# Cached attention: four sequences in one score tile, one score bank for the prompt's heads, a smaller descriptor ring

## The chip, the cores and the metric

The kernel runs on one core of a Trainium2 chip. The time is device microseconds (us) of one execution; the kernel is run several times and the median counts. One further execution was recorded by the hardware profiler; all rows below come from it.

The core's engines are named as in the profile: PE (TensorE's matrix products) and PEld (its weight loads), DVE (VectorE), ACT (ScalarE), POOL (GpSimd) and SP (SyncE, which here only starts transfers). Each runs its own list of instructions in the order in which the program wrote it, and they wait for each other by semaphores.

## The reference, cut to what matters

One step of a decoder layer for 512 prompt positions and for 8 sequences of 8 new positions each, 576 rows in all. A combined projection makes queries, keys, values, forget gates and the inputs of a convolution; attention with a bias from the forget gates and the convolution follow, then an output projection, an MLP and a gated embedding. The change touches the attention of the eight sequences, which reads 2048 cached positions each, through a table of pages of 128 positions:

```python
D_MODEL, SEQ, DEC_BATCH, DEC_SEQ, PAST_LEN, PAGE_SIZE = 2048, 512, 8, 8, 2048, 128
N_HEADS, HEAD_DIM = 8, 128
...
def fox_attention_sample(q, k_new, v_new, logf_new, k_past, v_past, logf_past):
    lp = logf_past.astype(jnp.float32)
    r_past = (lax.cumsum(lp, axis=1, reverse=True) - lp).transpose(0, 2, 1)
    cn = jnp.cumsum(logf_new, axis=1).transpose(0, 2, 1)
    s_past = jnp.einsum('bqhd,bkhd->bhqk', q, k_past).astype(jnp.float32) * scale
    s_past = s_past + cn[..., :, None] + r_past[..., None, :]
    s_new = jnp.einsum('bqhd,bkhd->bhqk', q, k_new).astype(jnp.float32) * scale
    s_new = s_new + cn[..., :, None] - cn[..., None, :]
    causal = jnp.arange(T)[None, :] <= jnp.arange(T)[:, None]
    s_new = jnp.where(causal, s_new, -jnp.inf)
    p = jax.nn.softmax(jnp.concatenate([s_past, s_new], axis=-1), axis=-1).astype(v_new.dtype)
    return (jnp.einsum('bhqk,bkhd->bqhd', p[..., :P], v_past)
            + jnp.einsum('bhqk,bkhd->bqhd', p[..., P:], v_new))
...
    k_past = cache_k[l][page_table].reshape(dec_b, past, N_HEADS, HEAD_DIM)
    v_past = cache_v[l][page_table].reshape(dec_b, past, N_HEADS, HEAD_DIM)
    lf_past = cache_logf[l][page_table].reshape(dec_b, past, N_HEADS)
    attn = fox_attention_sample(q, k, v, logf, k_past, v_past, lf_past)
```

The prompt's own attention is causal over its 512 positions with the same kind of bias; each head's result is normalised over its 128 channels before the output projection. All inputs are 32-bit floats.

## The kernel before

The program has two phases. Phase 2 (MLP, gate and final norm) is not touched; it and the output projection ahead of it begin at about 853 us. Phase 1 makes the combined projection and does everything else in its gaps.

**The projection.** `gemm_tile` makes one tile of 128 output channels for 576 rows: its weights come as four blocks of 128x512 (256 KB, tile `wraw`), are split into a high and a low part (`whi`, `wlo`) and go through 96 matrix products of 128x288 into a double bank `U` (`mm6`, L495). It pauses eight times; a stretch between two pauses, 12 products, is called a half here. At every pause `half()` (L367) is called. It first runs `flush_later()` (instructions held back on purpose, mainly exponentials on ACT), then lets the side work go one step: the queue `side` (convolution, `conv_norm`, the first `finish`) at every half, `att` (the prompt's heads, one after the other) at odd halves, and at even halves a credit grows by `DEC_RATE`; whenever it passes 1, the cached attention goes one step. So about every fourth half has a cache step. When the tiles are through, a drain loop alternates what is left with the projection of the embedding (`ple`, L1126).

**The cached attention** (`decode`, L795) has 16 units: two groups g of four heads, times eight sequences b. A unit has four steps, one for a chunk c of 512 positions (four pages). Rows of a score tile are 32 per head, of which eight (the sequence's queries) are meant; the other 24 hold queries of neighbours and are not used. A step issues, in this order:

- four transposes of the previous step's probabilities `dp` into bank `T` (L825), which ACT copies, eight columns of 32 only, to a 128x128 tile `PTs` (L826);
- a product of a selector `selU` with the table `R` (L838), which writes the bias of the 512 positions into bank `S`; the selector of the next unit is made by ACT at every fourth step (`unit_selector`, L871);
- 16 products of the queries `q_s` (as 32-column weights) with the cached keys `k`, added into `S` (L842);
- DVE's read of `S`, which adds the query's own bias, writes `dp` and gives the row maximum (L846), and its negation (L848); the exponential on ACT is put on `later` (L850);
- transfers on the SP queue for steps ahead (`load`, L802): two key tiles and two value tiles of 512 KB, each as two transfers of 256 KB with the page number read from the table. Five key tiles and four value tiles can be held;
- 16 products (32 records in the profile) of `PTs` with the cached values `v` of the step before the previous one, into a quarter of bank `O` (L863).

At a unit's last step `unit_end` (L877) merges the four chunks by their maxima, a 128x128 sum `uoc`, and POOL writes it to memory (`oc`, L892). The generator takes 66 steps.

**`finish(g)`** (L894) adds the eight new positions for a group of four heads: scores in bank `S` or `O`, their softmax, one transpose, products with the new values `v_s` for each sequence by itself (32 per round of four, L964), the merge with `oc` read back from memory, the norm, transposes of each sequence's 128x128 result (L984), and ACT's eight-column copies to `att_s` (L986). For g = 0 this goes in two rounds of four sequences beside the projection, for g = 1 in one round of eight in the drain.

**The prompt's heads** (`prompt_head`, L714): for each of four query blocks, `scores` (three products into `S`, DVE's read, a late exponential), `turned` (transposes to `T`, ACT's copy `pT`) and `values` (products into `S`, read twice by ACT, L752 and L753). It pauses nine times, once per odd half.

PSUM, the matrix products' memory, has eight banks of 128x512: two for `S`, one for `T`, one for `O`, two pairs for `U`.

Of the kernel before, what the change touches and what calls it, by code (L numbers as in the profile page):

```python
# [28 lines left out]
DEC_RATE = 0.485  # L29
# [6 lines left out]
C_ID, C_SELH, C_UM, C_CM, C_BM = 0, 128, 256, 272, 280  # L36
C_KEEP = 288
C_TRIU, C_SLOW, C_MASK = 288, 416, 544
C_SELG = 672
C_SEL16 = C_SELG + 256  # L40
# [3 lines left out]
C_T2 = C_TRIS + 32  # L44
C_END = C_T2 + 64


def const_pack():
# [8 lines left out]
    for r in range(128):  # L57
        h4 = r % 4
        c[r, C_SELH + h4 * 32:C_SELH + h4 * 32 + 32] = 1.0
        c[r, C_UM + r // 8] = 1.0  # L60
        g = C_SELG + r // 64 * 128 + h4 * 32
        c[r, g:g + 32] = 1.0
# [5 lines left out]
    q = p % 32  # L68
    for k in range(8):
        c[:, C_CM + k] = np.where((q < 8) & (k <= q), 0.0, NEG)  # L70
    for r in range(64):
        for qq in range(8):
            c[r, C_TRIS + qq] = (r % 8) <= qq
        c[r, C_BM + r // 8] = 1.0
        for k in range(64):
            c[r, C_T2 + k] = (r % 8) <= (k % 8)
# [66 lines left out]
class Kern:  # L143
# [28 lines left out]
    def row_rsqrt(self, ps, pool, dg, acc, out, n):  # L172
# [13 lines left out]
        for o, m in ((0, 512), (512, 64)):  # L186
            yield
            nc.tensor.matmul(pt[:, :m], self.ones, dg[:, o:o + m], start=True, stop=True)
            nc.scalar.activation(out[:, o:o + m], pt[:, :m], AF.Copy)
# [19 lines left out]
    heads = keys = 0  # L209
# [4 lines left out]
    def build(self):  # L214
        tc, nc, a = self.tc, self.nc, self.a
        with ExitStack() as top:
# [8 lines left out]
            self.oc = [dram.tile([128, 8, 128], F32, name=f"oc{j}") for j in range(2)]  # L225
# [17 lines left out]
    def phase1(self):  # L243
# [10 lines left out]
        ps_, pt_, po_, pu = Q("ps", 2), Q("pt", 1), Q("po", 1), Q("pu", 2)  # L254
# [3 lines left out]
        O_ = lambda: po_.tile([128, 512], F32, name="O", tag="O")  # L258
        U_ = lambda: pu.tile([128, 2, 512], F32, name="U", tag="U")
        self.S_, self.T_, self.O_, self.U_ = S_, T_, O_, U_  # L260

# [38 lines left out]
        self.selH, self.um, self.cm, self.bm = kc(C_SELH, 128), kc(C_UM, 16), kc(C_CM, 8), kc(C_BM, 8)  # L300
# [40 lines left out]
        self.att_s = c1.tile([128, 8, 64], F32, name="att_s")  # L341
        self.ysum = c1.tile([128, NR], F32, name="ysum")
        self.mlu = c1.tile([128, 2, 16], F32, name="mlu")
        self.PTs = []
        for i in range(2):
            t = c1.tile([128, 152], F32, name=f"PTs{i}")
            nc.gpsimd.memset(t[:, 128:], 0.0)
            self.PTs.append(t)
        self.PTm = c1.tile([64, 4, 56], F32, name="PTm")
        nc.gpsimd.memset(self.PTm, 0.0)  # L350
# [16 lines left out]
        def half():  # L367
# [8 lines left out]
            step(side)  # L376
            if odd:
                step(att)
                return
            D["credit"] += DEC_RATE  # L380
            if D["credit"] >= 1.0:
                D["credit"] -= 1.0
                if next(D["dec"], self) is self and D["mid"] is None:
# [3 lines left out]
                    side.append(self.finish(1, O_, O_, D["mid"]))  # L387
# [74 lines left out]
        while att or fq:  # L462
# [3 lines left out]
            step(att)  # L466
            next(ple, None)
            if n != 4:
                step(fq)
# [57 lines left out]
    def f_proj(self, wf, bfb):  # L527
# [57 lines left out]
        LBv = LB.rearrange("p (g h) b -> p g h b", g=2)  # L585
        LD = sm.tile([64, 2, 8, 2, 4], F32, name="LD")
# [24 lines left out]
        for h in range(4):  # L611
            nc.tensor.matmul(t[32 * h:32 * h + 32, :16].rearrange("p (g b) -> p g b", g=2), cp[:64, C_TRIS:C_TRIS + 32],
                             LBv[:, :, h, :], start=True, stop=True)
        self.cns = c1.tile([128, 16], F32, name="cns")
        nc.vector.tensor_copy(self.cns, t[:, :16])
        t = self.S_()
        nc.tensor.matmul(t[:, :64], LD.rearrange("p g b i h -> p (g b i h)"), cp[:64, C_T2:C_T2 + 64], start=True, stop=True)
        self.Rn = c1.tile([128, 64], F32R, name="Rn")
# [1272 lines left out]
```

## Time and profile before

| what | us |
| --- | --- |
| median of three runs | 2761.66 (2754.88 to 2769.64) |
| span of the profiled execution | 2757.2 |
| start, first projection tiles, biases: 0 to 119 | 119.0 |
| projection with cached attention and heads: 119 to 745 | 626.0 |
| last tiles, first `finish`, last cache steps: 745 to 812 | 67.0 |
| drain with the last `finish`: 812 to 853.2 | 41.2 |
| output projection and phase 2: 853.2 to the end | 1904.0 |

The span is the profiled execution's own time; it lies 4.5 us below the median of the runs. The mean clock granted to TensorE is 0.99 of full speed in the last stage and 1.00 in the others. In that last stage the DMA engines moved 167 GB/s and were busy for 0.54 of the time; in the stage from 119 to 745 us it was 291 GB/s and 0.87.

A row of a group names line, engine, operation, output and inputs, shape and count, then busy time in us and the mean of one in ns, then the engine's idle time just before these instructions and what ended most of it. In a timeline row the first number is the start and the second the duration. A matrix product's duration holds the latency of the pipeline, so that two neighbours overlap in the list; the distance of their starts is what the first one costs.

### The profile page before, as it was taken

To read this page: it belongs to the slowest core of one execution; us is meant where nothing else is said; L and a number is where in the kernel's file an instruction comes from. 1 tells how busy PE (TensorE), PEld (TensorE's weight loads), DVE (VectorE), ACT (ScalarE), POOL (GpSimd) and SP (SyncE) were. 2 spreads that over 40 slices of the span, in tenths; PEclk is the share of its full clock that TensorE was granted. 3 is DMA by queue.
4 is the path that set the end of the run, shared out by engine and by line. 5 is a ranking of instruction groups with operands and counts; after the bars stand their busy time and mean duration, and the time that the engine had idled before them with its cause. 6 is when DMAs were issued, how large, how long until landed. Compare 5 with 4: busy or idle time off the path is not lost.

```text
span 2757.2 us, 57342 instructions
## 1 busy us (share of the span) xinstructions
PE 2692.2 (98%) x22217; PEld 2599.2 (94%) x22217; DVE 2094.4 (76%) x3718; ACT 1211.7 (44%) x1841; POOL 524.1 (19%) x927
## 2 busy tenths in 40 slices
PE   8999999999999999999999999989999999998997
PEld 8988889998888999999999999989999999998997
DVE  5677777766555447888888888889888888887676
ACT  4233334345644324444444444545444444444554
POOL 1177776731100000000000000100000000000110
PEclk9999999999999999999999999999999999999999
DMA  4688888988736455444444444665565665655675
GB/s 153 211 285 293 279 291 289 296 296 303 267 130 202 141 201 178 141 140 142 143 143 142 140 137 142 213 173 169 163 191 156 175 175 166 184 171 180 198 243 172
DMA packets 239332, 538.44 MB, mean 195 GB/s; under 512 B 25842, under 2 KB 26739, under 8 KB 239059
## 3 DMA queue, kind: packets, MB, share of 16 engines
q1 hardware_dynamic: 171410, 329.06, 37.0%
q0 software_dynamic: 34112, 144.75, 16.7%
q10 hardware_dynamic: 33536, 60.96, 6.9%
q8 instruction: 174, 2.85, 0.4%
q14 instruction: 100, 0.81, 0.1%
HBM read 442.67 MB, written 92.01 MB: 194 GB/s over the span
## 4 chain that ended last, share of the span: by engine, by line
PE 51%; issue 4%; DVE 2%; DMA 1%; ACT 0%; POOL 0%; DVEq 0%; ACTq 0%; POOLq 0%
PE P L1539 15%; PE P L1540 15%; PE P L1541 15%; PE P L1607 2%; PE P L1609 2%; PE P L1608 2%; DVE w2l L152 1%; DMA xs<-x 1%; DMA x<-c 0%; ACT w2h L149 0%; DVE xs L1478 0%; DVE w2r L1763 0%; DVE x L1595 0%; DVE w2r L1764 0%; DVE w2r L1762 0%
## 5 line engine op out<-in xcount | busy, mean ns | idle before, releaser
L1539 PE MATMUL P<-xs,w2h 128*128 128x288 f32 x3584 | 1065.3, 297 | 15.2 <-DVE c L1656 6.8
L1540 PE MATMUL P<-xs,w2h 128*128 128x288 f32 x3584 | 1062.8, 297 | 4.2 <-DVE xs L152 4.2
L1541 PE MATMUL P<-xs,w2l 128*128 128x288 f32 x3584 | 1058.7, 295 | 2.5 <-DVE w2l L152 2.5
L149 ACT ACTIVATE w2h<-w2r 128x896 fp32r<-128x896 f32 (+1 forms) x632 | 556.1, 889 | 718.8 <-PE P L1540 416.8
L152 DVE TENSOR_TENSOR w2l<-w2r,w2h 128x896 fp32r<-128x896 f32 (+1 forms) x632 | 637.4, 1011 | 215.1 <-ACT w2h L149 213.5
L1539 PEld LDWEIGHTS P<-xs,w2h 128*128 128x128 f32 x3584 | 677.0, 189 | 20.7 <-DVE c L1656 9.4
L1540 PEld LDWEIGHTS P<-xs,w2h 128*128 128x128 f32 x3584 | 678.4, 189 | 6.6 <-DVE xs L152 6.3
L1541 PEld LDWEIGHTS P<-xs,w2l 128*128 128x128 f32 x3584 | 677.6, 189 | 4.3 <-DVE w2l L152 4.0
L495 PE MATMUL U<-xh,whi 128*128 128x288 f32 x1792 | 400.8, 305 | 2.6 <-ACT whi L123 1.3
L495 PE MATMUL U<-xh,wlo 128*128 128x288 f32 x1792 | 384.0, 296 | 1.7 <-DVE wlo L129 1.7
L495 PE MATMUL U<-xl,whi 128*128 128x288 f32 x1792 | 383.4, 295 | 1.8 <-DVE xl L328 1.7
L495 PEld LDWEIGHTS U<-xh,whi 128*128 128x128 f32 x1792 | 287.6, 189 | 23.4 <-issue 16.9
L495 PEld LDWEIGHTS U<-xl,whi 128*128 128x128 f32 x1792 | 287.9, 188 | 2.8 <-DVE xl L328 2.8
L495 PEld LDWEIGHTS U<-xh,wlo 128*128 128x128 f32 x1792 | 288.1, 188 | 2.4 <-DVE wlo L129 2.4
L123 ACT ACTIVATE whi<-wraw 128x512 fp32r<-128x512 f32 x224 | 141.2, 630 | 279.4 <-PE U L495 146.3
L129 DVE TENSOR_TENSOR wlo<-wraw,whi 128x512 fp32r<-128x512 f32 x224 | 160.3, 716 | 94.7 <-ACT whi L123 93.4
L1036 DVE SCALAR_TENSOR_TENSOR y<-ue,cv,y 128x512 f32<-128x512 f32 x240 | 183.4, 764 | 4.2
L1762 DVE TENSOR_TENSOR w2r<-w2r 128x512 f32<-128x512 f32 (+1 forms) x273 | 177.5, 650 | 4.9 <-DMA w2r<-in_w_down 4.9
L1037 POOL TENSOR_SCALAR cvt<-us,cv 128x64 f32<-128x64 f32 x240 | 168.5, 702 | 21.8
L1607 PE MATMUL P<-xs,w2h 128*128 128x288 f32 x512 | 151.8, 297 | 1.1 <-ACT c L1655 1.1
L1609 PE MATMUL P<-xs,w2l 128*128 128x288 f32 x512 | 151.0, 295 | 1.1 <-DVE w2l L152 1.0
L1608 PE MATMUL P<-xs,w2h 128*128 128x288 f32 x512 | 150.8, 295 | 0.0
(378 smaller groups left out, 2978.6 us busy)
## 6 DMA issues: line engine op xcount, KB each, us to landing
k<-in_cache_kv SPq DMA_DIRECT2D x256, 256.0 KB, 4.9
v<-in_cache_kv SPq DMA_DIRECT2D x256, 256.0 KB, 4.6
w2r<-in_w_up SPq DMA_DIRECT2D x127, 512.0 KB, 4.0
w2r<-in_w_down SPq DMA_DIRECT2D x112, 512.0 KB, 4.0
wraw<-in_w_main ACTq DMA_DIRECT2D x156, 256.0 KB, 5.0
xs<-di POOLq DMA_DIRECT2D x32, 1008.0 KB, 6.1
w2r<-in_w_gate SPq DMA_DIRECT2D x60, 512.0 KB, 4.4
x<-c POOLq DMA_DIRECT2D x48, 576.0 KB, 7.2
```

The lines of the kernel that those rows point to most:

```text
L149: self.nc.scalar.activation(out, in_, AF.Copy, **kw)
L152: self.nc.vector.tensor_tensor(out, in_, f(hi), ALU.subtract)
L495: self.nc.tensor.matmul(u[:, r, :HR], w, x[:, r * HR:(r + 1) * HR], start=first and n == 0, stop=last and n == 2)
L1036: nc.vector.scalar_tensor_tensor(y, ue[:, j:j + NPR], w, y, ALU.mult, ALU.add)
L1037: nc.gpsimd.tensor_scalar(t, us[:, :, j:j + 8], w, None, ALU.mult)
L1539: nc.tensor.matmul(o, hi[:, ia, :], s.hi[:, ib, :], start=(i == 0), stop=False)
L1540: nc.tensor.matmul(o, hi[:, ia, :], s.lo[:, ib, :], start=False, stop=False)
L1541: nc.tensor.matmul(o, lo[:, ia, :], s.hi[:, ib, :], start=False, stop=(i == n - 1))
L1607: nc.tensor.matmul(o, hi[:, ia, :], s.hi[:, kh, rows], start=first and kh == 0, stop=False)
L1608: nc.tensor.matmul(o, hi[:, ia, :], s.lo[:, kh, rows], start=False, stop=False)
L1609: nc.tensor.matmul(o, lo[:, ia, :], s.hi[:, kh, rows], start=False, stop=last and kh == 1)
L1762: lambda: V(w[:, :, 4:6, :], w[:, :, 0:1, :].broadcast_to([128, m, 2, 128]), w[:, :, 1:3, :], ALU.add),
```

## The change

**Four sequences share a score tile.** A step still has the keys of 512 positions and one group of four heads, but they are one page each of four sequences (key tiles) and four pages of the running group's sequences (value tiles). Four steps fill one tile of a bank `D` of their own: `q_s` is laid out with zeros between the sequences (160 columns for four of them), so that 32 columns of weights place one sequence's eight queries in its eight rows of a head's 32 and add nothing to the other rows. Selector, DVE's read, exponential, transposes and ACT's copies (now all 512 columns, `PT`) stand only in every fourth step; keys and values are multiplied in every step as before. There are four groups of (four heads, four sequences) with four chunks each; the generator takes 68 steps. The value products add four steps' worth into the four quarters of `O`; `merge` then takes from each quarter the rows of one sequence (a mask `rm`) into an accumulator in SBUF, `oacc`, scaled by a running maximum and sum `mlu`. There are no spills to memory.

**`finish`** works on 2 x 256 columns for both groups of sequences at once: scores in 16 columns, two transposes before the values, 16 records of products with `v_s`, two transposes after it. Both calls have the same form; g = 1 uses the banks `D` and `O`. `PTs`, `PTm`, `selG`, `unit_selector` and `unit_end` are gone; the four selectors `selU` are made once in `small_operands`.

**The prompt's heads** have one bank `S` instead of two (the other is `D`). They are advanced at every half instead of every odd one; most pauses are doubled, and `values` comes one pause later than `turned` and `scores` of its round. The transpose of `v_s` goes to `T`, and `pT` has two buffers. The drain loop advances them twice per pass.

**The rest.** `DEC_RATE` goes from 0.485 to 0.495. The program's scratch for the descriptors of the transfers that POOL starts is set to 8192 bytes; before, the default stood. The past bias uses `D` and `O` in turn, and `row_rsqrt` takes a new bank for each of its two products.

```diff
-DEC_RATE = 0.485
+DEC_RATE = 0.495
...
-        ps_, pt_, po_, pu = Q("ps", 2), Q("pt", 1), Q("po", 1), Q("pu", 2)
+        ps_, pt_, po_, pd_, pu = Q("ps", 1), Q("pt", 1), Q("po", 1), Q("pd", 1), Q("pu", 2)
...
-        self.q_s = c1.tile([128, 8, 88], F32, name="q_s")
-        nc.gpsimd.memset(self.q_s[:, :, 64:], 0.0)
+        self.q_s = c1.tile([128, 8, 2, 160], F32, name="q_s")
+        nc.gpsimd.memset(self.q_s, 0.0)
...
             step(side)
+            step(att)
             if odd:
-                step(att)
                 return
             D["credit"] += DEC_RATE
...
-                    side.append(self.finish(1, O_, O_, D["mid"]))
+                    side.append(self.finish(1, D_, O_))
...
             step(att)
+            self.flush_later()
             next(ple, None)
+            step(att)
             if n != 4:
...
+        self.selU = c1.tile([128, 4, 128], F32R, name="selU")
+        for i in range(4):
+            nc.scalar.activation(self.selU[:, i, :], self.selH, AF.Copy, scale=self.um[:, i:i + 1])
...
+    def q_of(self, h, b):
+        o = b % 4 * 32
+        return self.q_s[:, h, b // 4, o:o + 32]
...
         scores(0)
-        yield
+        for _ in range(2):
+            yield
         turned(0)
         scores(1)
-        yield
+        for _ in range(2):
+            yield
...
-        t = self.S_()
+        t = self.T_()
         nc.tensor.transpose(t[:64, :128], v[:, NPR:], self.ident)
         nc.scalar.activation(self.v_s[:, h, :], t[:64, :128], AF.Copy)
         self.heads += 1
-        yield
+        for _ in range(2):
+            yield
         for qt in range(4):
-            values(qt, vn)
             if qt < 3:
                 turned(qt + 1)
             if qt < 2:
                 scores(qt + 2)
+            yield
+            values(qt, vn)
             if qt == 3:
...
-                g, b = n // 64, n // 8 % 8
+                G, c, w, j = n // 32, n // 8 % 4, n // 2 % 4, n % 2
                 t = dec.tile([128, 2, 4, 128], F32, name="kv"[i], tag="kv"[i] * 2, bufs=(5, 4)[i])
-                for j in range(2):
-                    e = b * NPG + n % 8 * 2 + j
+                for x in range(2):
+                    b, pg = (w, 2 * j + x) if i == 0 else (2 * j + x, w)
+                    e = (G % 2 * 4 + b) * NPG + c * 4 + pg
                     r = nc.sync.value_load(self.pti[0:1, e:e + 1])
-                    nc.sync.dma_start(t[:, j].rearrange("p h c -> p (h c)"),
-                                      a["cache_kv"][bass.ds(r, 1), g, :, 512 * i:512 * i + 512].rearrange("o p c -> p (o c)"))
+                    nc.sync.dma_start(t[:, x].rearrange("p h c -> p (h c)"),
+                                      a["cache_kv"][bass.ds(r, 1), G // 2, :, 512 * i:512 * i + 512].rearrange("o p c -> p (o c)"))
...
-        for n in range(66):
+        s = o = mu = p = None
+        al, ls = {}, {}
+        one = lambda name: sm.tile([128, 1], F32, name=name, tag=name)
+        for n in range(68):
             if n == 0:
                 load(0, 5)
-                selU = {0: self.unit_selector(0)}
                 yield
-            if 1 <= n < 65:
-                m = n - 1
+            sc, w = n // 4, n % 4
+            G, c = sc // 4, sc % 4
+            if n >= 4 and w == 0:
                 t = self.T_()
                 for i in range(4):
-                    nc.tensor.transpose(t[:, i * 128:i * 128 + 128], ps[m][:, i * 128:i * 128 + 128], self.ident)
-                nc.scalar.activation(self.PTs[m % 2][:, :128].rearrange("p (a q) -> p a q", q=8),
-                                     t.rearrange("p (a q) -> p a q", q=32)[:, :, :8], AF.Copy)
-                del ps[m]
+                    nc.tensor.transpose(t[:, i * 128:i * 128 + 128], p[:, i * 128:i * 128 + 128], self.ident)
+                for i, m in ((0, 128), (128, 512)):
+                    nc.scalar.activation(self.PT[:, i:m], t[:, i:m], AF.Copy)
             if n < 64:
-                u, c = n // 4, n % 4
-                g, b = u // 8, u % 8
-                if c == 0:
-                    mx = sm.tile([128, 4], F32, name="dmx", tag="dmx")
-                    l4 = sm.tile([128, 4], F32, name="dl4", tag="dl4")
-                    units[u] = [mx, l4, None]
-                mx, l4, _ = units[u]
-                s = self.S_()
-                nc.tensor.matmul(s, selU[u], self.R[:, c * 512:c * 512 + 512], start=True, stop=False)
+                if w == 0:
+                    s = self.D_()
+                    nc.tensor.matmul(s, self.selU[:, G, :], self.R[:, c * 512:c * 512 + 512], start=True, stop=False)
                 for i in range(2):
                     kt = tiles[0][2 * n + i]
                     for h in range(4):
                         nc.tensor.matmul(s[32 * h:32 * h + 32, i * 256:i * 256 + 256].rearrange("p (a b) -> p a b", a=2),
-                                         self.q_s[:, 4 * g + h, b * 8:b * 8 + 32], kt[:, :, h, :],
-                                         start=False, stop=(i == 1))
-                p = ps[n] = dec.tile([128, 512], F32, name="dp", tag="dp", bufs=2)
-                nc.vector.tensor_scalar(p, s, self.cns[:, u:u + 1], None, ALU.add, ALU.max, accum_out=mx[:, c:c + 1])
-                nm = sm.tile([128, 1], F32, name="dnm", tag="dnm")
-                nc.vector.tensor_scalar(nm, mx[:, c:c + 1], -1.0, None, ALU.mult)
-                self.later.append(lambda p=p, nm=nm, l=l4[:, c:c + 1]:
-                                  nc.scalar.activation(p, p, AF.Exp, bias=nm, accum_out=l))
-                if c == 2 and u < 15:
-                    selU = {u: selU[u], u + 1: self.unit_selector(u + 1)}
+                                         self.q_of(G // 2 * 4 + h, G % 2 * 4 + w), kt[:, :, h, :],
+                                         start=False, stop=(w == 3 and i == 1))
+                if w == 3:
+                    p = dec.tile([128, 512], F32, name="dp", tag="dp")
+                    mx = one("dmx")
+                    nc.vector.tensor_scalar(p, s, self.cns[:, G:G + 1], None, ALU.add, ALU.max, accum_out=mx)
+                    new = self.mlu[:, 0, G:G + 1]
+                    if c == 0:
+                        nc.vector.tensor_copy(new, mx)
+                        ls[sc] = self.mlu[:, 1, G:G + 1]
+                    else:
+                        al[sc], ls[sc] = one("dal"), one("dls")
+                        V(mx, mx, new, ALU.max)
+                        V(al[sc], new, mx, ALU.subtract)
+                        nc.vector.tensor_copy(new, mx)
+                    nm = one("dnm")
+                    nc.vector.tensor_scalar(nm, mx, -1.0, None, ALU.mult)
+
+                    def late(p=p, nm=nm, l=ls[sc], d=al.get(sc)):
+                        nc.scalar.activation(p, p, AF.Exp, bias=nm, accum_out=l)
+                        if d is not None:
+                            nc.scalar.activation(d, d, AF.Exp)
+                    self.later.append(late)
                 load(0, 2 * n + 6)
-            if n >= 2:
-                m = n - 2
-                u, c = m // 4, m % 4
-                if c == 0:
-                    units[u][2] = self.O_()
-                o, PT = units[u][2], self.PTs[m % 2]
-                for i in range(4):
+            if n >= 4:
+                m = n - 4
+                if w == 0:
+                    o = self.O_()
+                for r in range(4):
                     for h in range(4):
-                        e = (i * 4 + h) * 8
-                        nc.tensor.matmul(o[32 * h:32 * h + 32, c * 128:c * 128 + 128], PT[:, e:e + 32],
-                                         tiles[1][2 * m + i // 2][:, i % 2, h, :], start=(i == 0), stop=(i == 3))
-                if c == 3:
-                    self.unit_end(u, *units.pop(u))
-            load(1, 2 * n + 2)
+                        nc.tensor.matmul(o[32 * h:32 * h + 32, r * 128:r * 128 + 128], self.PT[:, w * 128 + h * 32:w * 128 + h * 32 + 32],
+                                         tiles[1][2 * m + r // 2][:, r % 2, h, :], start=(w == 0 and r == 0), stop=(w == 3 and r == 3))
+                if w == 3:
+                    self.merge(m // 16, m // 4 % 4, o, al.pop(m // 4, None), ls.pop(m // 4))
+            load(1, 2 * n - 2)
             load(0, 2 * n + 7)
             yield
...
+    def merge(self, G, c, o, al, l):
+
+        nc = self.nc
+        acc = self.oacc[:, G, :]
+        if c == 0:
+            nc.vector.tensor_scalar(acc, o[:, :128], self.rm[:, 0:1], None, ALU.mult)
+        else:
+            lu = self.mlu[:, 1, G:G + 1]
+            nc.vector.scalar_tensor_tensor(lu, lu, al, l, ALU.mult, ALU.add)
+            nc.vector.tensor_scalar(acc, acc, al, None, ALU.mult)
+        for r in range(c == 0, 4):
+            nc.vector.scalar_tensor_tensor(acc, o[:, r * 128:r * 128 + 128], self.rm[:, r:r + 1], acc, ALU.mult, ALU.add)
+        self.groups += c == 3
+
...
+        oc = part("foc")
+        V(oc, self.oacc[:, 2 * g:2 * g + 2, :], wide(w1), ALU.mult)
+        yield
+        while self.heads < 4 * g + 4:
+            yield
+        u = S()
+        for i in range(2):
+            for h in range(4):
+                nc.tensor.matmul(u[32 * h:32 * h + 32, i * 128:i * 128 + 128], pT[:, 128 * i + 32 * h:128 * i + 32 * h + 32],
+                                 self.v_s[:, 4 * g + h, :], start=True, stop=True)
+        on = part("fon")
+        V(on, u[:, :256].rearrange("p (a d) -> p a d", a=2), wide(w2), ALU.mult)
+        V(on, on, oc, ALU.add)
+        for i in range(2):
+            nc.scalar.activation(oc[:, i, :], on[:, i, :], AF.Square, accum_out=t8[:, i:i + 1])
+        yield
+        nc.vector.tensor_scalar(t8, t8, 1.0 / 128.0, EPS, ALU.mult, ALU.add)
+        yield from self.rsqrt_steps(sm, m, t8, [128, 2], "f")
+        V(on, on, wide(m), ALU.mult)
         yield
         t = T()
+        for i in range(2):
+            nc.tensor.transpose(t[:, i * 128:i * 128 + 128], on[:, i, :], self.ident)
...
-    nc = bacc.Bacc("TRN2", target_bir_lowering=False, num_devices=1)
+    nc = bacc.Bacc("TRN2", target_bir_lowering=False, num_devices=1, dynamic_dma_scratch_size=8192)
```

More of the change, by code (lines that the diff above doesn't have):

```diff
@@ L57, in const_pack @@
     for r in range(128):
[L58 to L62, printed above, removed]
+        o = C_SELH + r % 4 * 32 + r // 8 % 4 * 8
+        c[r, o:o + 8] = 1.0
+        c[r, C_UM + r // 32] = 1.0
+        c[r, C_RM + r // 8 % 4] = 1.0
+        for a in range(2):
+            c[r, C_UB + 8 * a + 4 * a + r // 8 % 4] = 1.0
     c[:8, C_M16] = 1.0
@@ L771, in prompt_head @@
         self.heads += 1
-        yield
+        for _ in range(2):
+            yield
         for qt in range(4):
-            values(qt, vn)
             if qt < 3:
@@ L910, in finish @@
-        while self.keys < 4 * g + 4:
+        s2 = lambda name: sm.tile([128, 2], F32, name=name, tag=name, bufs=1)
+        part = lambda name: self.cnp.tile([128, 2, 128], F32, name=name, tag="cn", bufs=3)
+        wide = lambda t: t[:, :, None].broadcast_to([128, 2, 128])
+        pause = lambda: iter(range(0 if self.draining else 3))
+        while self.keys < 4 * g + 4 or self.groups < 2 * g + 2:
             yield
@@ L993, in evac_cin @@
+        for j in range(2):
+            nc.sync.dma_start(self.am[2 * g + j][:, :, NPR:], att[:, 2 * j:2 * j + 2, :])
     def evac_cin(self, u, i, ct, hb):
```

196 lines of the change are left out of this document (65 added, 131 removed).

## The prediction

> **What bounds the kernel now.** I read the page first for the busiest engine, then busy time by stage, then TensorE's timeline inside one cache step, then what TensorE and the SP queue wait for.
>
> ```profile
> PE 2692.2 (98%) x22217; PEld 2599.2 (94%) x22217; DVE 2094.4 (76%) x3718; ACT 1211.7 (44%) x1841; POOL 524.1 (19%) x927
> ```
>
> TensorE is busy for 98% of the span, and no other engine passes 76%. Instructions leave TensorE in the order written, so one that is taken out shortens the span by the distance between its start and the next start, unless the next one then waits.
>
> The cached attention runs from 119 to 776 us. Its windows (columns: stretch and length, then PE, PEld, DVE, ACT, POOL busy with counts, granted clock, DMA share, GB/s):
>
> ```profile
> 120.00:540.00 420.00, 413.13 (x4507) 373.56 (x4505) 314.02 (x605) 142.32 (x295) 299.01 (x527) 1.00 0.87 288
> 540.00:780.00 240.00, 235.62 (x2491) 213.10 (x2483) 152.27 (x425) 124.72 (x295) 56.50 (x105) 1.00 0.80 271
> 680.00:700.00 20.00, 19.08 (x173) 17.27 (x172) 13.97 (x37) 16.79 (x33) 3.22 (x6) 1.00 0.98 339
> ```
>
> The clock is granted in full, TensorE is busy for 98% here too, but the DMA engines are at 0.87, so they are second in line. One cache step in TensorE's timeline (start us, us, engine line):
>
> ```profile
> 410.44 0.43 PE L495 MATMUL U<-xh,wlo 128*128 128x288 f32 x2
> 410.70 0.60 PE L825 MATMUL T<-ident,dp 128*128 128x128 f32 x4
> 411.06 0.48 PE L838 MATMUL S<-R,selU 128*128 128x512 f32 x1
> 411.47 1.07 PE L842 MATMUL S<-k,q_s 128*32 128x256 f32 x16
> 412.35 1.06 PE L863 MATMUL O<-v,PTs 128*32 128x128 f32 x32
> 413.34 0.53 PE L495 MATMUL U<-xh,whi 128*128 128x288 f32 x2
> 413.71 0.42 PE L495 MATMUL U<-xl,whi 128*128 128x288 f32 x2
> ...
> 419.84 0.60 PE L825 MATMUL T<-ident,dp 128*128 128x128 f32 x4
> ```
>
> The second column holds pipeline latency, so I count start to start: transposes 0.36, selector 0.41, keys 0.88, values 0.99, together 2.64 us. The projection's pairs follow each other every 0.265 us (410.44 to 410.70); a half tile is six pairs, 1.6 us. Four halves and one step are 9.14 us (410.70 to 419.84).
>
> **What the change takes off TensorE.** (1) All four sequences share one score tile, so selector and transposes stand in every fourth step: 16 of 64, 48 sets gone. Keys (16 records) and values (32) stay at 64 sets each. A set is 0.36 + 0.41 = 0.77 us. But the keys now follow the projection directly, and the turn from 128-column to 32-column work isn't free. The trace has that turn once:
>
> ```profile
> 756.34 0.43 PE L495 MATMUL U<-xh,wlo 128*128 128x288 f32 x2
> 756.70 1.08 PE L964 MATMUL S<-v_s,PTm 64*32 64x128 f32 x32
> 757.71 0.53 PE L495 MATMUL U<-xh,whi 128*128 128x288 f32 x2
> ```
>
> The next start is due at 756.60 and comes at 756.70: 0.10 us stay. I take 48 x 0.67 = 32.2 us. Without any turn it would be 37.0.
>
> ```profile
> 411.46 0.59 PEld L842 LDWEIGHTS S<-k,q_s 128*32 128x32 f32 x16 [0.25 <-issue]
> ```
>
> The weight load of the keys sat idle for 0.25 us at that turn behind the selector; if all of it stays in all 48 steps, the gain is 48 x 0.52 = 25.0. These are the two ends, and the turn that was seen behind the projection itself decides between them. The Trainium skill (TensorEngine Tiling (Array Packing), Key Properties) says that changing the tiling mode drains the array, which speaks for the lower end; the page gives no price, so the sum by it is the 25.0, and the trace shows a smaller loss, 0.10, at the same kind of turn.
>
> (2) The last finish, in the drain (812 to 853 us):
>
> ```profile
> 816.32 1.95 PE L964 MATMUL U<-v_s,PTm 64*32 64x128 f32 x64
> ...
> 839.17 1.04 PE L984 MATMUL U<-ident,fon 128*128 128x128 f32 x8
> ...
> 841.23 2.21 PE L1126 MATMUL U<-praw,wple 128*128 128x288 f32 x8 [1.02 <-ACT att_s L986]
> ```
>
> The value products ran from 816.32 to 818.20, 1.88 us; 16 of 64 records remain, 0.47, saving 1.4. Transposes and the wait behind them took 2.06 us (839.17 to 841.23); two of eight remain, about 0.26, and they go to a bank that the next matmul doesn't want, saving 1.8. Together 3.2.
>
> (3) The first finish had two rounds of value products, 1.01 us each (756.70 to 757.71); a quarter remains, saving 1.5. These waits of TensorE stood around it, 3.8 us, because one T bank served the finish, the heads and the cache:
>
> ```profile
> 764.02 0.63 PE L984 MATMUL T<-ident,fon 128*128 128x128 f32 x4 [0.41 <-DVE fon L980]
> 765.63 0.66 PE L825 MATMUL T<-ident,dp 128*128 128x128 f32 x4 [0.97 <-ACT att_s L986]
> 785.46 0.63 PE L984 MATMUL T<-ident,fon 128*128 128x128 f32 x4 [1.93 <-DVE l L744]
> 787.00 0.55 PE L741 MATMUL T<-ident,p 128*128 128x128 f32 x3 [0.47 <-ACT att_s L986]
> ```
>
> **What it adds.** (4) One S bank in place of two. In the new order of instructions five places have two users of one bank between two halves: channel sums and ldg of conv_norm ahead of a head's values, the finish's new scores ahead of a head's scores, pe ahead of a head's transposes, the finish's values ahead of a head's values. The second user waits for an eviction:
>
> ```profile
> L846 DVE TENSOR_SCALAR_CACHE_REDUCE dp<-S,cns 128x512 f32<-128x512 f32 x64 | 47.9, 748 | 66.2 <-PE S L842 66.2
> L752 ACT ACTIVATE o<-S,l 128x128 f32<-128x128 f32 x32 | 11.7, 365 | 26.3 <-PE S L749 26.3
> L753 ACT ACTIVATE S<-S,l 128x128 f32<-128x128 f32 x32 | 10.7, 334 | 0.0
> ```
>
> At 0.36 to 0.83 us of eviction, and nothing if it is early, I take 0.8 for each, 4.0 in all (ends 0 and 10). Elsewhere the next user of S comes a half later, 1.6 us, and the eviction (0.83 by DVE, or 0.70 plus 0.2 for the sum on ACT) fits under it while its engine is on time. DVE's 66.2 us of idle in front of its 64 evictions say that it mostly waits for TensorE; for the times it is late I add 2 (0 to 10). If an eviction is late, the PE instruction that waits holds the projection behind it, which all others wait for.
>
> (5) Off TensorE nothing goes onto the path. DVE loses 48 evictions of 748 ns and ACT 48 exponentials; the merges replace unit_end's on the same rows of O. The value products of a first step in four wait for ACT's copy as all did, under selector and keys (1.3 us). The larger memset stands on POOL in the first 60 us, where q_s is not yet written. The rate 0.495 needs 69 calls, done at even half 140 of 144; 0.485 needed 67, done at 139. The spills of 64 KB and their loads vanish. The smaller ring I cost at nothing (rival 3).
>
> (6) The cover. Loads are issued in order on SP; a step brings eight cache transfers of 256 KB and two of weights, 2.6 MB. What TensorE and SP waited for (us, times, longest), 100 to 860 us:
>
> ```profile
> PE O L863 <- DMA v<-in_cache_kv: 6.5, 10, 1.7
> ...
> SPq L811 <- DMA wraw<-in_w_main: 133.9, 68, 5.3
> ...
> SPq L811 <- PE S L842: 44.8, 26, 7.2
> ```
>
> SP mostly waits for transfers, not for a buffer that TensorE holds, so it has little lead. The mean step falls from 4.12 halves x 1.6 + 2.64 = 9.2 to 4.04 x 1.6 + 0.75 x 1.97 + 0.25 x 2.64 = 8.6 us, and the load rises from 288 to 308 GB/s, the share from 0.87 to 0.93. The chip does 339 for a while, so it can be had, but value waits should grow. Ends: they vanish (-7) or eat half the step's gain (+16); near the middle, a bit above: +9.
>
> **Sum.** -32.2 - 3.2 - 1.5 - 3.8 + 4.0 + 2 + 9 = -25.7 us on a span of 2757.2. The median of the runs lies 4.5 above that span; I put the same difference on it: 2761.7 - 25.7 = 2736.
>
> **Rivals.** (1) The transfers set the pace. First and last of 44 value sets, 43 steps apart:
>
> ```profile
> 121.31 1.06 PE L863 MATMUL O<-v,PTs 128*32 128x128 f32 x32
> ...
> 539.09 1.05 PE L863 MATMUL O<-v,PTs 128*32 128x128 f32 x32
> ```
>
> 417.8 / 43 = 9.72 us a step, more than the 9.14 of TensorE's work, with SP waiting for transfers. If 9.72 is a floor, those 43 steps gain nothing and, at 0.08 halves fewer each, leave 43 x 0.08 x 1.6 = 5.5 us of projection for later. Left over: 21 of 64 x 32.2 = 10.6, and items 2 to 4 (-2.5): -13.1 + 5.5 + 2 = -5.6, some -9 with ACT's shorter queue: 2753. For it: the waits for v. Against: SP waits on weights that ACT issues at TensorE's own pace, and 339 GB/s was seen.
>
> (2) Slower: the single bank. The heads take S 72 times (nine each). If every take waits for a whole eviction, about 0.85 us, as it would with DVE or ACT one instruction late, that is 61 us: 2736 - 2 + 61 = 2795. It decides from about 0.55 us a take (25.7 + 13.8 over 72). Against it stand the 1.6 us between takes.
>
> (3) The halved ring holds POOL back, where its transfers are chained:
>
> ```profile
> L1462 POOL DMA_DIRECT2D xs<-x x8 | 4.3, 533 | 19.0 <-DMA x<-c 19.0
> ```
>
> The chain of waits shows one of them (start us, us):
>
> ```profile
> 2476.74 3.97 DMA xs<-x
> ```
>
> Eight loads of the gate's operands, each 4 us later, are 32 on top of the sum: 2736 + 32 = 2768. An issue takes 0.53 us and transfers are several us apart, so it is unlikely.
>
> **How the numbers follow.** My sum 0.62, rival 1 0.20, rival 2 0.10, rival 3 0.04, something else 0.04. The likeliest gives 2736, by itself 2718 to 2748 (turn 25 to 37, banks 0 to 20, value waits -7 to +16). The range to hold 8 in 10 takes in rival 1: 2718 to 2758. I call 0.5%, 13.8 us, what can be told from no change. Faster by more: nine tenths of the first case, a third of the second, half the rest: 0.65. Slower: rival 2 and a little: 0.11. Same: 0.24.
>
> **What would show it.** Right: T<-ident,dp x64 and the selector x16; the projection's last pair to the first key 0.37 us; steps near 8.5 us from 130 us on; the drain 3 us shorter; after 853 us the same length. Wrong: waits of O on DMA v near 25 us or more with steps at 9.7 (rival 1); waits of S<-vn,pT or S<-cb for DVE or ACT beyond 15 us (rival 2); a longer last part with POOL idle longer ahead of xs (rival 3).

## The result, and the profile after

The changed kernel takes 2754.99 us (median of five runs, 2750.36 to 2757.27) against 2768.58 us of the kernel before (five runs, the three that the prediction knew and two more, 2754.88 to 2770.36): a ratio of 0.9945, with a 95% interval of 0.993 to 0.9959. By the ratio it is faster by 0.55%, some 15 us (the two medians are 13.6 us apart), where 25.7 us (0.93%) were forecast. The interval, 0.41 to 0.70%, holds the 0.5% from which on the prediction spoke of a change. The time lies in the range given, but not in the likeliest case's own 2718 to 2748: the sign was right, the size about 0.6 of the forecast.

The profiled execution has a span of 2748.6 us. Busy time by engine, then the windows that were shown of before:

```profile
PE 2669.2 (97%) x21873; PEld 2571.8 (94%) x21873; DVE 2044.5 (74%) x3553; ACT 1156.3 (42%) x1696; POOL 510.4 (19%) x906
```

```profile
120.00:540.00 420.00, 403.51 (x4384) 360.88 (x4380) 294.52 (x518) 106.75 (x199) 292.52 (x527) 1.00 0.87 292
680.00:700.00 20.00, 20.00 (x213) 17.60 (x212) 14.77 (x35) 14.90 (x31) 5.01 (x9) 1.00 0.95 322
```

From 120 to 540 us TensorE is idle for 16.5 us, against 6.9 before, and the transfers run at 292 GB/s where 308 were forecast. A cache step without a selector in TensorE's timeline:

```profile
348.70 0.43 PE L493 MATMUL U<-xh,wlo 128*128 128x288 f32 x2
349.06 1.07 PE L847 MATMUL D<-k,q_s 128*32 128x256 f32 x16
349.95 0.62 PE L878 MATMUL O<-v,PT 128*32 128x128 f32 x16
351.80 0.43 PE L878 MATMUL O<-v,PT 128*32 128x128 f32 x8 [1.23 <-DMA v<-in_cache_kv]
```

The step begins with the keys 0.36 us after the last pair, but its values wait for a transfer. The first and the 44th set of values, as before:

```profile
136.47 1.06 PE L878 MATMUL O<-v,PT 128*32 128x128 f32 x32
...
540.76 1.36 PE L878 MATMUL O<-v,PT 128*32 128x128 f32 x32
```

404.3 / 43 = 9.40 us a step, against 9.72 before and 8.6 forecast. The first sets are 8.45 us apart (136.47, 144.92, 153.38 us); the first wait for v comes at 207.8 us. Transposes and selector by line, with their counts:

```profile
L837 PE MATMUL T<-ident,dp 128*128 128x128 f32 x64 | 10.0, 281 | 0.0
L843 PE MATMUL D<-R,selU 128*128 128x512 f32 x16 | 7.9, 492 | 0.0
```

There are four transposes a set, so both stand 16 times. What TensorE waited for (us, times, longest; 100 to 860 us):

```profile
PEld O L878 <- DMA v<-in_cache_kv: 25.7, 35, 2.7
PE O L878 <- DMA v<-in_cache_kv: 16.1, 25, 2.4
PE T L798 <- DVE o L792: 6.1, 6, 1.8
PE S L772 <- DVE v L691: 2.6, 3, 0.9
PE S L189 <- DVE ldg L183: 1.2, 1, 1.2
PE S L753 <- ACT vacc L190: 0.7, 1, 0.7
PE S L753 <- DVE fon L963: 0.7, 1, 0.7
PE O L878 <- ACT PT L839: 0.6, 1, 0.6
PE S L753 <- DVE ysum L1063: 0.6, 1, 0.6
PE T L745 <- ACT fpT L951: 0.5, 1, 0.5
```

The waits for v rose from 6.5 us (10 times) to 16.1 (25 times); the third and fourth rows (a head's closing transposes, and the transposes of its values) stand in no term of the prediction. The mark for what follows is the start of the output projection, 853.2 us before:

```profile
835.74 4.29 PE L1117 MATMUL U<-praw,wple 128*128 128x288 f32 x17
839.65 0.64 PE L493 MATMUL U<-xh,whi 128*128 128x288 f32 x2
```

It comes 13.6 us earlier. From there to the end it is 1909.0 us, against 1904.0. That part is the same program, and in the runs below it takes 1900 to 1915 us with no relation to what was edited; so the mark tells more than the span. A mark is still that of one profiled execution: two of the kernel before, with and without the small ring, are 4.5 us apart.

### The profile page after: what moved, and what is told of

It reads as the page before. It is cut to its first block, busy times and chain, and to the rows that moved or that the text cites. A ratio compares the mean times of both kernels' runs of the same rounds, so it can differ in the third digit from the quotient of the medians.

```text
span 2748.6 us, 56300 instructions
## 1 busy us (share of the span) xinstructions
PE 2669.2 (97%) x21873; PEld 2571.8 (94%) x21873; DVE 2044.5 (74%) x3553; ACT 1156.3 (42%) x1696; POOL 510.4 (19%) x906
## 4 chain that ended last, share of the span: by engine, by line
PE 50%; issue 4%; DVE 3%; DMA 1%; ACT 1%; POOL 0%; DVEq 0%; ACTq 0%; POOLq 0%
PE P L1531 14%; PE P L1530 14%; PE P L1532 14%; PE P L1598 2%; PE P L1600 2%; PE P L1599 2%; DVE w2l L152 1%; DMA xs<-x 1%; ACT w2h L149 0%; DVE w2r L1754 0%; DVE w2r L1753 0%; DVE xs L152 0%; DVE w2r L1755 0%; DVE xs L1469 0%; DVE c L1662 0%
## 5 line engine op out<-in xcount | busy, mean ns | idle before, releaser
L1028 POOL TENSOR_SCALAR cvt<-us,cv 128x64 f32<-128x64 f32 x240 | 160.0, 667 | 22.2
```

## The experiments

The expectations speak of the last product of the embedding, which ends some 0.3 us behind the mark; in one run, e4, the two differ. Ratios are to runs of the kernel before that were taken beside each, with 95% intervals.

| run | mark, us | median us | ratio |
| --- | --- | --- | --- |
| before | 853.2 | 2768.58 | |
| changed | 839.7 | 2754.99 | 0.9945 (0.993 to 0.9959) |
| e1, half of the value bytes | 814.8 | 2722.06 | 0.9832 (0.9814 to 0.9849) |
| e2, no page lookups | 813.6 | 2726.92 | 0.9851 (0.9832 to 0.987) |
| e3, values started by ACT | 831.3 | 2735.21 | 0.9873 (0.9855 to 0.9891) |
| e4, a head's end two halves later | 840.8 | 2752.08 | 0.9943 (0.9924 to 0.9962) |
| e5, each lookup used twice | 814.9 | 2725.06 | 0.9854 (0.9835 to 0.9873) |
| e6, e5 and two heads' waits | 808.7 | 2718.28 | 0.9834 (0.9817 to 0.985) |
| e7, before without lookups | 849.3 | 2757.42 | 0.9969 (0.9956 to 0.9983) |
| e8, the old cadence on one bank | 853.7 | 2755.8 | 0.9964 (0.9948 to 0.9981) |
| e9, before with the small ring | 857.7 | 2767.75 | 0.9998 (0.9982 to 1.0014) |
| e10, two lookups | 943.1 | 2854.8, one run | |

**Why the values are late: bytes, or SP's pace.** SP's timeline in the changed kernel (start us, from the first start to the last of a group, count):

```profile
333.98 2.90 SPq L821 DMA_DIRECT2D v<-in_cache_kv  x4
337.38 6.68 SPq L821 DMA_DIRECT2D k<-in_cache_kv  x4
```

Four starts and their lookups take 3.40 us, 0.85 each; the lookup's own record (TENSOR_LOAD on SP) takes 0.27 us in the median. Eight starts are 6.8 us a step, and the waits for landings come on top. Four runs tell the two theories apart.

```diff
-a["cache_kv"][bass.ds(r, 1), G // 2, :, 512 * i:512 * i + 512]
+a["cache_kv"][bass.ds(r, 1), G // 2, :, 512 * i:512 * i + (512, 256)[i]]
...
```

> The changed kernel, but each value transfer brings two of its four heads (128 KB in place of 256 KB) and the value products of the other two heads read the same columns: half of the value bytes are left out, a quarter of the cache's. The number of transfers on SP is the same. In the changed kernel TensorE waits 16.1 us (25 times) for v by its matrix products' row and 25.7 us (35 times) by its weight loads' row, and the last embedding product ends at 840.0 us. If the bytes set the pace (rival 1 of the prediction), both rows fall under 4 us and that end comes near 826. If SP's pace of starting transfers sets it (8 per step, each with a lookup of the page), the rows stay above 12 and 18 us and the end stays within 838 to 842.

```diff
-r = nc.sync.value_load(self.pti[0:1, e:e + 1])
...
-a["cache_kv"][bass.ds(r, 1), ...
+a["cache_kv"][e:e + 1, ...
```

> The changed kernel, but the page numbers are constants of the program: the lookup in the page table on SP is left out, so that other pages are read; bytes and number of transfers are the same. If SP's pace of starting transfers is the limit, the waits for v fall under 5 us in both rows and the last embedding product ends near 827 in place of 840.0. If the bytes are the limit, nothing moves by more than 3 us.

Both took away every wait of the value products for v, and the mark fell to 814.8 and 813.6. e2 keeps all bytes and moves them faster than the changed kernel:

```profile
120.00:330.00 210.00, 210.00 (x2341) 191.88 (x2340) 154.58 (x255) 54.02 (x90) 159.51 (x283) 1.00 0.92 319
```

319 GB/s, where the changed kernel moves 288 in the same stretch: bytes were not the limit. (e2 reads other pages than the table names; e5 and e10 below read the right ones.) What SP waited for from 120 to 540 us, in the changed kernel, in e1 and in e2:

```profile
SPq L821 <- DMA wraw<-in_w_main: 92.8, 56, 4.2
SPq L821 <- PE D L847: 5.4, 5, 4.2
```

```profile
SPq L821 <- DMA wraw<-in_w_main: 40.7, 28, 3.1
SPq L821 <- PE D L847: 31.4, 17, 5.5
```

```profile
SPq L820 <- PE D L846: 120.1, 46, 6.2
SPq L820 <- DMA v<-in_cache_kv: 46.7, 36, 3.2
```

In the changed kernel SP hardly ever waits for TensorE to free a buffer: it is behind. In e2 that is its longest wait: it is ahead. e1 missed both expectations. It has as many starts, but the shorter transfers land sooner (3.5 us from issue to landing in the median, against 4.5), and a start that waits for an earlier landing waits less (92.8 to 40.7 us). SP's time is starts plus landings, and taking enough from either is enough. Taken alone, e1 would have spoken for the bytes.

e3 gives the value transfers to ACT's queue, one at each half:

```diff
+if self.vq:
+    self.vq.popleft()[1]()
...
+q = (nc.sync, nc.scalar)[i]
+r = q.value_load(self.pti[0:1, e:e + 1])
+q.dma_start(tiles[i][n][:, x]...
...
```

> The changed kernel, but the value transfers are started from ACT's queue, one at each half, and only the key transfers from SP: same bytes, same lookups, two queues. If SP's pace is the limit, the waits for v fall under 6 us, and the last embedding product ends between 826 and 832 (four lookups a step on ACT may hold up the splitting of the weights, where a few us may come back). If the bytes are the limit, the waits stay and the end is at 840 or later.

The waits for v are gone. But ACT's work now waits for landings of k and v (50.2 and 32.8 us of its idle time from 100 to 860 us), and TensorE waits for ACT's copy of the probabilities; the mark came to 831.3, within what was expected:

```profile
PE O L891 <- ACT PT L850: 7.8, 5, 3.4
```

The Trainium skill (DMA: Bandwidth & Descriptors, Issuing engines are not separate DMA queues) says that starting transfers from several engines saves only the sequencer's time, which is usually small beside the transfer. One start is small here too, 0.85 us against a landing after 4.5; eight of them, 6.8 us in a step that was to take 8.6, were not.

e10 doubles the suspected cost in place of removing it:

```diff
+y = nc.sync.value_load(self.pti[0:1, e:e + 1])
...
-a["cache_kv"][bass.ds(r, 1), G // 2, ...
+a["cache_kv"][bass.ds(r, 1), bass.ds(y - r + G // 2, 1), ...
```

> The changed kernel with a second lookup of the same page number ahead of each transfer (the difference of the two, zero, is added to another index): same bytes, same transfers. A start on SP takes 0.84 us at its closest in the changed kernel and 0.37 without the lookup; with two it should take about 1.25. If SP's pace is the limit, a step of eight starts needs 10 us and some 2 for landings, against 9.2 us now: 64 steps later by 1 to 3 us each, the last embedding product at 900 to 1000 us in place of 840, waits for v above 60 us. If the bytes are the limit, it ends within 838 to 848.

```profile
318.81 4.19 SPq L822 DMA_DIRECT2D k<-in_cache_kv  x4
323.99 4.21 SPq L822 DMA_DIRECT2D v<-in_cache_kv  x4
```

```profile
PE O L879 <- DMA v<-in_cache_kv: 76.4, 67, 2.7
```

Four starts take 5.18 us, 1.30 each, and the mark of this single run moves to 943.1 with the same bytes, though a transfer lands sooner after its issue than in the changed kernel (v in 3.3 us in the median, against 4.5): SP's pace is the cause.

**The same limit in the kernel before**, with the edit of e2:

> The kernel before, but the page numbers are constants (the lookup on SP is left out, so that other pages are read). TensorE's waits for v in it were 6.5 us by the matrix products' row and 10.4 us by the weight loads', about 9.7 us over the normal distance. If SP's pace is behind these too, they vanish and the last embedding product ends near 844 in place of 853.6. Then the change gains 30 us (844 to 814) where SP doesn't hold it back, against 13.5 us as it is. If not, the end stays within 852 to 855.

The mark falls from 853.2 to 849.3, between the two expectations, though the value products no longer wait for v at all. A mark has a scatter of this size, as e9 shows, the kernel before with the ring alone:

```diff
-nc = bacc.Bacc("TRN2", target_bir_lowering=False, num_devices=1)
+nc = bacc.Bacc("TRN2", target_bir_lowering=False, num_devices=1, dynamic_dma_scratch_size=8192)
```

> The kernel before with the smaller descriptor ring alone (8192 bytes). The prediction costs it at nothing: ratio 1.000 within 0.002, the last embedding product at 853 to 857 us, as long a way from there to the end as before (1903.6 us) within 4. By rival 3 POOL is held up in phase 2 and the time grows by some 30 us.

The ring changes no time (ratio 0.9998). Its mark is 857.7, just past the expected 857, and the granted clock of the first 95 us, first in the profile of before and then in e9's, tells where some of the difference lies:

```profile
0.00:95.00 95.00, 86.27 (x633) 80.17 (x634) 61.66 (x133) 38.10 (x56) 15.77 (x40) 1.00 0.41 141
```

```profile
0.00:95.00 95.00, 85.76 (x611) 78.30 (x611) 60.83 (x131) 37.49 (x55) 15.74 (x40) 0.97 0.39 137
```

So lookups cost the kernel before 4 to 8 us by the marks (0.31% or 8.6 us by the ratio), and the changed one 26 (839.7 to 813.6).

**The heads.** e4 puts the end of a head later:

```diff
-if not self.draining:
+for _ in range(1 if self.draining else 3):
     yield
 t = self.T_()
```

> The changed kernel, but a head's last transposes come two halves later while the projection runs, as late as before the change. My theory: the doubled cadence halved the time between a head's last values and these transposes, and TensorE waits for DVE's normalised o (6.1 us by its row, 7 of 8 heads). Then this row falls under 2.5 us (the one in the drain stays) and the last embedding product ends near 835 in place of 840.0. The rival: a head that ends two halves later makes the next one late, the chain of heads is longer, and the end stays within 839 to 842.

```profile
840.00 1.11 PE L798 MATMUL T<-ident,o 128*128 128x128 f32 x4 [3.70 <-DVE o L792]
840.76 0.83 PE L493 MATMUL U<-xh,whi 128*128 128x288 f32 x2
```

The waits beside the projection went, and the last embedding product ended at 835.2 as my theory has it; but then the last head's transposes wait 3.70 us in the drain, and the output projection starts at 840.8. It came out as the rival has it, and the time didn't change: a head now takes 17 halves where two tiles have 16, so that each head ends later than the one before it, up to the drain.

e8 brings back the heads' order and cadence of before (the other halved pauses and the drain's single advance are left out here):

```diff
-step(att)
 if odd:
+    step(att)
     return
...
 for qt in range(4):
+    values(qt, vn)
     if qt < 3:
         turned(qt + 1)
     if qt < 2:
         scores(qt + 2)
-    yield
-    values(qt, vn)
...
```

> The changed kernel with one score bank, but the heads in the order and cadence of before: one advance at each odd half, values ahead of the next turn and scores, and one advance in each pass of the drain. Then two takes of the one bank S stand in one gap, twice in each head (values, then scores). By the price of the prediction, an eviction and its signals, 0.85 us for each, it is 16 x 0.85 = 14 us slower than the changed kernel where the waits count, less the 7 us of the closing transposes, which have their time back: last embedding product near 847. If the bank is never waited for (ACT's reads are early), it ends near 833.

```profile
PE S L728 <- ACT S L755: 11.0, 16, 1.5
PE T L967 <- DVE fon L963: 2.9, 1, 2.9
```

The 16 expected takes wait, 0.69 us each by this row, and a wait for finish's transposes was not foreseen. The mark is 853.7, behind the expected 847. By the rows of waits some 8 us of the 14 are accounted for; the granted clock from 745 to 812 us, 0.92 against 1.00 in the changed kernel, is an estimated 5 more (0.08 x 67). The run time doesn't show the loss: the ratios, 0.9964 and 0.9945, have overlapping intervals, and behind its mark e8 takes 1900.4 us, less than any other run. So rival 2's wait, where two users of one bank stand in one gap, is shown by the row and not by the time; the new cadence keeps them apart.

**A faster version.** e5 keeps the page number for the value transfer of the same page:

```diff
-r = nc.sync.value_load(self.pti[0:1, e:e + 1])
+r = pages.pop(e) if i else nc.sync.value_load(self.pti[0:1, e:e + 1])
+if i == 0:
+    pages[e] = r
```

> The changed kernel, but the page number that SP looks up for a key transfer is kept in a register and used again for the value transfer of the same page four steps later: the same transfers and bytes, four lookups a step in place of eight. Without any lookup the waits for v were gone and the last embedding product ended at 814 us, in the changed kernel it ends at 840.0. If the lookups are what holds SP back, half of them gone is enough to take most of the waits away: both rows of waits for v under 6 us, the end between 814 and 822, about 20 us faster than the changed kernel. If the pace of starting transfers is set by the landings that SP waits for (each start waits until an earlier transfer, often one of weights, has landed), it gains less than 10 us and the rows stay above 8 us.

Half of the lookups are enough: no waits for v, and the mark at 814.9. SP now waits mostly for TensorE to free a buffer (88.7 us from 120 to 540 us, against 5.4 in the changed kernel). e6 adds the heads' edits, kept to 16 halves:

```diff
-if not self.draining:
+for _ in range(0 if self.draining else 2):
     yield
...
+yield
 v = hb["v"]
...
 self.heads += 1
-for _ in range(2):
-    yield
+yield
```

> The changed kernel with the page numbers used twice, a head's last transposes one half later (16 halves a head, as many as two tiles have), and the transposes of a head's values one half after its values are found, with one pause less behind them. If the three costs are separate, they add: waits for v under 6 us, PE T L798 <- DVE o and the waits for DVE v gone (7.0 and 3.0 us over their normal distance), the last embedding product at 806 to 813 us, the time about 1.5% below the kernel before. If a later end of a head makes the chain of heads longer, the end stays at the value of the run with the page numbers alone.

```profile
PE T L798 <- DVE o L792: 1.8, 1, 1.8
```

One wait for o is left, in the drain; the mark is 808.7. e6 computes all that the reference does and is 1.66% faster than the kernel before.

## Why the forecast was right in sign and too large

- **(1) Selector and transposes: right.** 16 sets are left. The turn from the projection to the keys is 349.06 - 348.70 = 0.36 us where a pair takes 0.265: 0.10 us, as taken. It is 0.35 or 0.36 at each such turn from 120 to 520 us. That a drain of the array makes these 0.10 us isn't shown; the lower end, 25.0, is not borne out.
- **(2), (3) finish: right as far as shown.** No wait for its closing transposes stands in the rows of the changed kernel any more. The drain, from the first embedding product to the mark, is 40.1 us against 41.4, so 1.3 us shorter in place of 3.2: a wait of 1.8 us for the last head's closing transposes stands in it now. The two terms were not tried alone.
- **(4) One bank: right, and a little dear.** Four of the five places named have a row: channel sums (`ysum`) 0.6, ldg (`vacc`, which ACT writes from that bank) 0.7, the finish's values (`fon`) 0.7 and pe (`fpT`) 0.5, together 2.5 us against 4.0. The finish's new scores are not waited for. The row of L189 is no wait for the bank: TensorE waits there for `ldg` itself, as it did before for 0.4 us. The 2 us for a late DVE don't show. Rival 2's wait is real (e8), but the order of instructions avoids it.
- **A term that was missing.** Heads advance twice as often, and most pauses were doubled, but not the one ahead of a head's closing transposes, and none was put in after its values are found. I looked at the new order for users of one bank, and not for how long a chain still had: values, ACT's squares, DVE's norm, transposes. It cost 6.1 + 2.6 us by the rows (0.7 of the second stood there before); e6 got 6.2 us of it back (814.9 to 808.7).
- **(6) The cover: the step that failed.** The prediction took the DMA engines for the second resource in line, compared 308 GB/s with the 339 seen, and added 9 us. What ran short was SP's own time: it counted what SP waits for, and no time for SP's starts and lookups themselves. Without lookups the change moves the mark from 849.3 to 813.6, by 35.7 us; the sum without term (6) was 34.7. With them it moves it by 13.6, or 18.0 against e9's mark. So the term is 18 to 22 us, not 9, and outside the ends given for it (-7 to +16). The run times say the same: 0.9851 / 0.9969 is 33 us, against 15 with lookups. That 35.7 comes so near to 34.7 is partly luck, since it holds the heads' waits, which no term has. Two rows of SP's timeline in the kernel before would have told it:

```profile
408.10 2.92 SPq L811 DMA_DIRECT2D k<-in_cache_kv  x4
411.59 4.06 SPq L811 DMA_DIRECT2D v<-in_cache_kv  x4
```

  Four starts in 3.49 us, 0.87 each, make 7.0 a step; the 133.9 us of waits for weights' landings, over 64 steps, add 2.1. By this estimate SP needs 9.1 us a step: less than the old step's 9.72, and more than the 8.6 forecast for the new one (8.82 in e2, where SP doesn't hold it back). The argument against rival 1, that the weights follow TensorE's pace, holds for the waits alone and not for the starts.
- **Rival 1** had the right queue of work and the wrong floor: the step went to 9.40 us, under its 9.72. It read the 0.58 us between 9.72 and 9.14 as waiting. But from 120 to 540 us TensorE was busy for 413.13 of 420 us before and for 403.51 after: 9.56 of the 9.72 us a step were work, the heads' products included, and 9.03 of the 9.40. The 9.14 were a step without a head's products, and the 8.6 left them out too. Its sum also seems to take the 2 us for DVE twice: -5.6 would then be -7.6. It gave a gain of 9 us and the sum one of 25.7; the 15 measured lie between.
- **Rival 3** fell: e9's ratio is 0.9998, and behind its mark it takes 2765.6 - 857.7 = 1907.9 us, within the 1900 to 1915 of all runs.

## What to carry to other kernels

When work is taken off the bounding engine, work out the next resource per step in each of its units: bytes, buffers, and also the time of the queue that starts the transfers, lookups and waits for landings included. A queue that, like SP here, hardly ever waits for a buffer that the bounding engine holds has no lead, however much bandwidth is left. When the cadence of a chain is changed, follow each chain to its end, and look at the pauses that were not scaled.

## What was not expected of the hardware

Waits cost a second time, by the clock. In e10 three waits stand close together (TensorE's timeline), and the windows behind them (PE busy, granted clock, DMA share, GB/s) show the granted clock at 0.50 for 4 us:

```profile
293.42 0.43 PE L879 MATMUL O<-v,PT 128*32 128x128 f32 x8 [1.06 <-DMA v<-in_cache_kv]
294.40 0.42 PE L879 MATMUL O<-v,PT 128*32 128x128 f32 x8 [0.56 <-DMA v<-in_cache_kv]
297.17 1.28 PE L879 MATMUL O<-v,PT 128*32 128x128 f32 x16 [2.35 <-DMA v<-in_cache_kv]
298.38 0.85 PE L493 MATMUL U<-xh,whi 128*128 128x288 f32 x2
299.03 0.68 PE L493 MATMUL U<-xl,whi 128*128 128x288 f32 x2
299.51 0.68 PE L493 MATMUL U<-xh,wlo 128*128 128x288 f32 x2
```

```profile
298.40:302.40 4.00, 4.00 (x21) 0.50 0.69 204
302.40:306.40 4.00, 4.00 (x31) 0.98 0.61 202
```

A pair of products takes 0.48 us in place of 0.265. The Trainium skill (TensorE: Matmul & The Clock Gate, HAM oscillation — how this bites in real kernels) gives as the rule that TensorE should have no idle gap above about 3.4 us. In e4 a wait of 3.70 us did it, as that rule has it: behind it a pair takes 0.48 us for about 5 us. In e10 no gap was longer than 2.35 us, and three of them, 4.0 us in 5, were enough: the trace agrees that idle time halves the clock, and not that it takes a single gap of that length. Nor do short gaps always do it: from 225 to 230 us in e10, three waits of 0.98, 0.28 and 1.44 us left the clock at 1.00. What decides between the two isn't shown.
